# A bidirectional RWKV-7 layer: full-height lo products in the lora-up, lora rows in another buffer, chunk-end stores on ScalarE's queue

## The chip, the cores and the metric

One Trainium2 chip, one of its cores. The metric is device time in microseconds (us) of one execution; the kernel before took 1825.01 us as the median of three runs (1819.26 to 1827.5). The traces are of one profiled execution each.

## The reference

A layer mixes 128 context tokens and 2048 latent tokens of 1024 channels. All tokens are normalised and modulated to `h`, and one projection gives eight groups of 512 channels. Four of them (r, k, v, g_a) feed an RWKV-7 scan in both directions, the other four a gated short convolution. What the change touches are the two low-rank ("lora") paths, the decay `w` and the in-context rate `a`, each with its own weights for each direction `e`:

```
lw = tanh(einsum('btd,edl->betl', hf, decay_down))          # 64 rows for each direction
w = decay_w0 + einsum('betl,elc->betc', lw, decay_up)
decay = exp(-exp(-softplus(-w) - 0.5))
la = einsum('btd,edl->betl', hf, iclr_down)
a = sigmoid(iclr_bias + einsum('betl,elc->betc', la, iclr_up))
...
S = S * w_t - s_kk (kk_t * a_t) + v_t k_t                   # one step of the scan
```

Then come a group norm, the gates, the output projection, a residual and a final norm.

## The kernel before

**Three phases.** Phase 1 projects everything and writes the operands of the scan to HBM; phase 2 runs the scans in chunks of 64 tokens; phase 3 is the output projection. Nearly all the change lies in phase 1.

**Phase 1.** Tokens lie in six blocks `j` of 384 columns (the last has 256), two blocks to a "third" (`THIRD`). In a third, the loop over the four channel groups `g` of 128 takes two turns: `turn(0, g)` runs `mixA` (k, r, both loras) and a part of the convolution, `turn(1, g)` runs `gateA` (v, g_a) and the rest. `load_w` brings one weight block and splits it into a high and a low part in a rounded fp32 type (`F32R`), and `dense` sums 24 matmuls over the three useful products of high and low parts. `part_sum` does the same with a block of ones (`pss`, `psb`).

**The lora rows.** `lora_down` makes, for each block, four tiles `lw`: index `which*2 + d` for the path `which` (0 decay, 1 rate) and the direction `d`. Of the 128 rows of a tile, the 64 of half `d` hold the high part of the lora rows and the other 64 their low part. ScalarE evacuates the product to `lf`; VectorE casts and subtracts it into `lw` (L563, L564). `lf` lies in the buffer with the tag `sq`, of which there is one; `mixA` holds it from the square of k (L348) to the last product that reads `kkn` (L403).

**The lora-up.** `lup(which)` makes one output tile `up` with two matmuls: the high part of the up-weights (both halves hold the same 64 rows) by all 128 rows of `lw` (L367), and the low part by the 64 high rows alone (L368). `mixA` calls it four times: w and a of direction 0, then of direction 1. That is 8 matmuls for each of 6 x 4 pairs of block and group, 24 groups of 8 and 192 in all. `load_up` splits the up-weights once, near the start.

**Stores.** `mixA` stores four operands for each direction (`spill`, L336) out of a tag `sp` with four buffers, and by L394 the decay at the end of each chunk, `pc`: 6 numbers in each of 128 rows. All go out through SP's queue, 48 of the `pc` kind. Loads go through SP too.

**Other buffers.** `smask` (L375 to L379) is the mask by which the running sums of the decay restart at every chunk. The shifted k, r and v lie in `ok`, `or` and `ov` (L328 to L330). `bsv` (L513) holds b times its gate; `pv` the rows of the vertical convolution and, in the first third, the gate rows. `q1`, two buffers, holds a scaled copy of k, r or v (L322) and of c (L457).

**What sets the order.** The framework's scheduler places all instructions of an engine in a fixed order, from the program order, the buffers and its own estimate. So a change of buffers moves instructions. HBM transfers of SP and ScalarE take turns on eight semaphores, so that a DMA can wait for the eighth DMA before it.

Of the kernel before, what the change touches and what calls it, by code (L numbers as in the profile page):

```python
# [6 lines left out]
F32 = mybir.dt.float32  # L7
F32R = mybir.dt.float32r
BF16 = mybir.dt.bfloat16
AF = mybir.ActivationFunctionType  # L10
ALU = mybir.AluOpType
# [38 lines left out]
def phase1(K):  # L50
    nc, tc, A, S = K.nc, K.tc, K.A, K.S
    V, G, P, T = nc.vector, nc.gpsimd, nc.scalar, nc.tensor
# [18 lines left out]
    V.tensor_copy(onr[:], ones[:])  # L71
    onf = cp.tile([128, 128], F32R, name="onf")
    V.tensor_scalar(onf[:], ones[:], 0.0, 1.0, ALU.mult, ALU.add)
    smask = ca.tile([128, 384], F32, name="smask")
    eps = cp.tile([128, 1], F32, name="eps")
    V.memset(eps[:], 1e-6)
    nln2 = cp.tile([128, 1], F32, name="nln2")
# [24 lines left out]
    def load_up():  # L102

        raw = ta_.tile([128, 2, 2, 512], F32, tag="x", name="upraw", bufs=1)
        for h in range(2):
            nc.sync.dma_start(raw[h * 64:h * 64 + 64], A["wup"].rearrange("n (d p) c -> p n d c", d=2))
        parts = ca.tile([128, 6, 512], F32R, tag="upx", name="ups")
        hi, lo = parts[:, 0:4].rearrange("p (n d) c -> p n d c", d=2), parts[:, 4:6]
        for n in range(2):
            V.tensor_copy(hi[:, n], raw[:, n])  # L110
            for d in range(2):
                r = slice(d * 64, d * 64 + 64)
                V.tensor_tensor(lo[r, n], raw[r, n, d], hi[r, n, d].bitcast(F32), ALU.subtract)
                up[n, d] = (hi[:, n, d], lo[:, n])

    kept = set()

# [196 lines left out]
    def shifted(ps, j, mi, g, nm, bufs=2):  # L314

        t0, n = BLK[j]
        lo = lat_off(j)
        R = (n - lo) // 64
        rp = rot(rawl, "raw")
        P.copy(rp[:, :R, 1:65], ps[:, lo:n].rearrange("p (r c) -> p r c", c=64))  # L320
        q1 = tp.tile([128, 384], F32, tag="q1", name=f"q1{nm}_{K.u()}", bufs=2)
        P.activation(q1[:, :n], ps[:, :n], AF.Identity, scale=dcol(D_MU1 + mi * 4 + g))  # L322
        s = tp.tile([128, 384], F32, tag="sh", name=f"sh{nm}_{K.u()}", bufs=2)
        G.tensor_tensor(s[:, lo:n].rearrange("p (r c) -> p r c", c=64), rp[:, :R, 0:64], rp[:, :R, 2:66], ALU.add)  # L324
        if lo:
            rc = rot(rawc, "rawc")
            P.copy(rc[:, 1:129], ps[:, 0:128])
            V.tensor_tensor(s[:, 0:128], rc[:, 0:128], rc[:, 2:130], ALU.add)  # L328
        o = ta_.tile([128, 384], F32, tag=f"o{nm}", name=f"o{nm}_{K.u()}", bufs=bufs)
        V.scalar_tensor_tensor(o[:, :n], s[:, :n], dcol(D_MUH + mi * 4 + g), q1[:, :n], ALU.mult, ALU.add)  # L330
        return o

# [5 lines left out]
    def mixA(g, j, ws, hh, lw, pre):  # L338

        t0, n = BLK[j]  # L340
        nch = n // 64
        tl = lambda tag, b=1: (tp if tag == "sg" else ta_).tile([128, 384], F32, tag=tag, name=f"{tag}_{g}_{j}_{K.u()}", bufs=b)
        wk, wr_ = ws
        psk, psr = pre or (None, None)

        kS = shifted(psk or dense(wk, hh, n, "k"), j, 1, g, "k", 1)
        sq = tl("sq")
        P.activation(sq[:, :n], kS[:, :n], AF.Square, scale=vcol(V_KK + g))  # L348
        pss = part_sum(onr, sq, n, f"s{g}_{j}")
        n2 = sq  # L350
        V.tensor_scalar(n2[:, :n], pss[:, :n], 1e-24, None, ALU.max)
        V.reciprocal(n2[:, :n], n2[:, :n])
        kk = tl("kk")
        P.activation(kk[:, :n], kS[:, :n], AF.Identity, scale=vcol(V_KK + g))
        kkn = n2
        V.tensor_tensor(kkn[:, :n], kk[:, :n], n2[:, :n], ALU.mult)
        rS = shifted(psr or dense(wr_, hh, n, "r"), j, 0, g, "r", 1)
        kds = []
        for d in range(2):
            rows = slice(d * 64, d * 64 + 64)  # L360
            cs = slice(g * 128, g * 128 + 128)

            def lup(which):
                ps = pmm.tile([128, 384], F32, tag="mm", name=f"up{which}_{K.u()}")
                hi, lo = up[which, d]
                x = lw[which * 2 + d]
                T.matmul(ps[:, :n], hi[:, cs], x[:, :n], start=True, stop=False)  # L367
                T.matmul(ps[:, :n], lo[rows, cs], x[rows, :n], start=False, stop=True)  # L368
                return ps

            psw = lup(0)
            t = tl("t", 2)
            P.activation(t[:, :n], psw[:, :n], AF.Tanh, bias=dcol(D_W0H + d * 4 + g), scale=0.5)
            V.tensor_scalar(t[:, :n], t[:, :n], -0.5 * DEC, -0.5 * DEC, ALU.mult, ALU.add)
            c = t  # L375
            if d == 0:
                V.tensor_tensor_scan(c[:, :n], smask[:, :n], t[:, :n], 0.0, ALU.mult, ALU.add)
            else:
                V.tensor_tensor_scan(c[:, :n][:, ::-1], smask[:, :n], t[:, :n][:, ::-1], 0.0, ALU.mult, ALU.add)  # L379
            pt = rot(pp[d], "pp")  # L380
            c3 = c[:, :n].rearrange("p (a b) -> p a b", b=64)
            P.activation(pt[:, :nch, 1 - d:65 - d], c3, AF.Exp)
            P.activation(c[:, :n], c[:, :n], AF.Exp, bias=nln2[:], scale=-1.0)
            psa = lup(1)
            ta = tl("ta", 2)
            P.activation(ta[:, :n], psa[:, :n], AF.Tanh, bias=dcol(D_IBH + d * 4 + g), scale=0.5)
            v3 = lambda x_: x_[:, :n].rearrange("p (a b) -> p a b", b=64)
            al = tl("sp", 4)
            V.tensor_tensor(v3(al), v3(kk), pt[:, :nch, d:64 + d], ALU.mult)
            spill(f"al{d}", g, j, al, "al")  # L390
            rh = tl("sp", 4)
            V.tensor_tensor(v3(rh), v3(rS), pt[:, :nch, 1 - d:65 - d], ALU.mult)
            spill(f"rh{d}", g, j, rh, "rh")
            nc.sync.dma_start(S[f"pc{d}"][g * 128:(g + 1) * 128, t0 // 64:t0 // 64 + nch], pt[:, :nch, 64 - 64 * d])  # L394

            kd = tl("kd", 2)
            P.activation(kd[:, :n], ta[:, :n], AF.Identity, bias=dcol(D_KA2 + g), scale=vcol(V_KA + g))
            V.tensor_tensor(kd[:, :n], kd[:, :n], kS[:, :n], ALU.mult)
            kap = tl("sp", 4)
            V.tensor_tensor(kap[:, :n], kd[:, :n], c[:, :n], ALU.mult)  # L400
            spill(f"ka{d}", g, j, kap, "kap")
            be = tl("sp", 4)
            V.scalar_tensor_tensor(be[:, :n], ta[:, :n], 1.0, kkn[:, :n], ALU.add, ALU.mult)  # L403
            V.tensor_tensor(be[:, :n], be[:, :n], c[:, :n], ALU.mult)
            spill(f"be{d}", g, j, be, "be")
            kds.append(kd)
        bs = kds[0]
        V.tensor_tensor(bs[:, :n], kds[0][:, :n], kds[1][:, :n], ALU.add)
        V.scalar_tensor_tensor(bs[:, :n], bs[:, :n], dcol(D_RKQ + g), rS[:, :n], ALU.mult, ALU.mult)
        psb = part_sum(onr, bs, n, f"b{g}_{j}")  # L410
        bsum = tl("bsum", 2)
        P.copy(bsum[:, :n], psb[:, :n])
        return bsum
# [86 lines left out]
    def gateB(g, j, ws, hh, conv):  # L500

        o, oc, back, m = conv
        t0, n = BLK[j]
# [6 lines left out]
        P.activation(sg[:, :n], psg[:, :n], AF.Tanh, scale=0.5)  # L510
        V.scalar_tensor_tensor(sg[:, :n], sg[:, :n], 1.0, psg[:, :n], ALU.add, ALU.mult)
        psb = dense(wb, hh, n, "b")
        bsv = tp.tile([128, 7, 64], F32, tag="bsv", name=f"bsv{g}_{j}", bufs=1)  # L513
        dst = S["mixT"][512 + g * 128:640 + g * 128]
        if lo:
            V.tensor_tensor(oc, oc, sg[:, 0:128], ALU.mult)
# [35 lines left out]
    def lora_down(j, wd, wi, pre):  # L552
        n = BLK[j][1]
        nm = j % 2
        lw = [ta_.tile([128, 384], F32R, tag=f"lw{i}_{nm}", name=f"lw{i}_{j}") for i in range(4)]
        for which, (w, fn) in enumerate(((wd, AF.Tanh), (wi, AF.Copy))):
            ps = pre[which] if pre else dense(w, hs[j], n, f"l{which}")
            f = ta_.tile([128, 384], F32, tag="sq", name=f"lf{which}_{j}", bufs=1)
            P.activation(f[:, :n], ps[:, :n], fn)
            for d in range(2):  # L560
                a, b = slice(d * 64, d * 64 + 64), slice(64 - d * 64, 128 - d * 64)
                t_ = lw[which * 2 + d]
                V.tensor_copy(t_[a, :n], f[a, :n])  # L563
                V.tensor_tensor(t_[b, :n], f[a, :n], t_[a, :n].bitcast(F32), ALU.subtract)  # L564
        return lw
# [7 lines left out]
    for t3, js in enumerate(THIRD):  # L573
# [5 lines left out]
        def prepare(j):  # L579
            if j not in hs:  # L580
                if t3 == 0:
                    pre[0] = psf[2:]
                    nc.sync.dma_start(smask[:], A["cst"][:, 128:512])
                run(make_h(j, xb[j]))
            lws[j] = lora_down(j, wd, wi, psf[:2] if j == 0 else None)

# [818 lines left out]
```

## Time and profile before

| what | value |
| --- | --- |
| the three runs | 1825.01 us median (1819.26 to 1827.5) |
| the profiled execution | 1824.67 us, of which span 1822.9 us |
| TensorE matmuls busy in the span (PE) | 1703.8 us, 93%, 13424 matmuls |
| VectorE (DVE) | 1216.1 us, 67% |
| ScalarE (ACT) | 822.2 us, 45% |
| GpSimd (POOL) | 584.5 us, 32% |
| mean TensorE clock granted | 0.968 |

PE is the array, PEld its weight loads, DVE VectorE, ACT ScalarE, POOL GpSimd and SPq the issue of SP's DMAs. A matmul's recorded duration overlaps the next one's, so pace is read from the distance of starts, not from durations. "Idle before" is the time an engine stood still ahead of an instruction, and the arrow names what ended it. The three thirds of phase 1 run from about 75, 410 and 745 us, and phase 2's first products start at 977 us.

### The profile page before, as it was taken

To read this page: it belongs to the slowest core of one execution; us is meant where nothing else is said; L and a number is where in the kernel's file an instruction comes from. 1 tells how busy PE (TensorE), PEld (TensorE's weight loads), DVE (VectorE), ACT (ScalarE), POOL (GpSimd) and SP (SyncE) were. 2 spreads that over 40 slices of the span, in tenths; PEclk is the share of its full clock that TensorE was granted. 3 is DMA by queue.
4 is the path that set the end of the run, shared out by engine and by line. 5 is a ranking of instruction groups with operands and counts; after the bars stand their busy time and mean duration, and the time that the engine had idled before them with its cause. 6 is when DMAs were issued, how large, how long until landed. Compare 5 with 4: busy or idle time off the path is not lost.

```text
span 1822.9 us, 35136 instructions
## 1 busy us (share of the span) xinstructions
PE 1703.8 (93%) x13424; PEld 1539.4 (84%) x13424; DVE 1216.1 (67%) x2285; ACT 822.2 (45%) x1583; POOL 584.5 (32%) x1089
## 2 busy tenths in 40 slices
PE   5899999998999999799999799899999999898998
PEld 2789889897999999699999788788888888776886
DVE  5875788756367756447764656678777878858433
ACT  4433454523144432333342366567666656543222
POOL 0011111111021110111110777867766676422221
PEclk8899999998999999899999899999999999998999
DMA  8787788755555656547668576568667765645442
GB/s 353 205 237 208 219 264 257 206 219 141 194 142 173 179 184 187 155 138 226 195 184 275 129 179 159 138 162 198 161 165 185 161 153 129 179 149 183 143 149 98
DMA packets 315817, 335.37 MB, mean 184 GB/s; under 512 B 166968, under 2 KB 263992, under 8 KB 301568
## 3 DMA queue, kind: packets, MB, share of 16 engines
q1 hardware_dynamic: 278928, 324.20, 61.3%
q10 hardware_dynamic: 35360, 4.46, 1.6%
q0 software_dynamic: 1360, 4.46, 0.7%
q8 instruction: 106, 1.74, 0.4%
q14 instruction: 63, 0.52, 0.1%
HBM read 221.22 MB, written 111.82 MB: 183 GB/s over the span
## 4 chain that ended last, share of the span: by engine, by line
PE 53%; DMA 17%; DVE 12%; POOL 8%; issue 5%; ACT 3%; SPq 1%; DVEq 0%; ACTq 0%; POOLq 0%
DMA scr_ops<-sp 5%; POOL zt L940 4%; PE psE L1012 4%; PE psu L1278 3%; PE psu L1279 3%; PE psu L1280 3%; POOL ztmp L937 3%; DMA wr<-in_win 3%; DMA ab<-scr_at 2%; PE psS L1059 2%; DMA w<-scr_q 2%; PE psG L898 2%; PE psF L898 2%; PE mmc L161 1%; PE mmc L163 1%
## 5 line engine op out<-in xcount | busy, mean ns | idle before, releaser
L940 POOL TENSOR_TENSOR zt<-zt,ztmp 128x30 f32<-128x30 f32 (+7 forms) x510 | 198.8, 390 | 38.9
L1012 PE MATMUL psE<-str,stl 128*128 128x128 f32 x1088 | 156.2, 289 | 11.3 <-DVE E L1013 10.1
L1012 PEld LDWEIGHTS psE<-str,stl 128*128 128x128 f32 x1088 | 136.0, 197 | 19.3 <-DVE E L1013 11.8
L937 POOL TENSOR_TENSOR ztmp<-ab,zt 128x60 f32<-128x60 f32 (+7 forms) x255 | 133.9, 525 | 18.6
L785 ACT COPY bd<-rr 64x512 f32<-64x512 f32 x136 | 83.9, 617 | 79.0 <-PE psF L898 26.6
L324 POOL TENSOR_TENSOR shk<-rawl 128x384 f32<-128x384 f32 (+1 forms) x24 | 21.1, 881 | 296.9 <-ACT rawl L320 296.9
L1013 DVE TENSOR_TENSOR E<-psE,msk 128x512 f32<-128x512 f32 x136 | 93.5, 688 | 29.0 <-PE psE L1012 26.8
L1025 PE MATMUL psY<-E,sv 128*64 128x64 f32 x1088 | 105.8, 234 | 0.7 <-DVE E L1013 0.4
L1059 PE MATMUL psS<-sv,E 128*64 128x64 f32 x1056 | 104.0, 236 | 2.2 <-DVE sv L1071 2.1
L898 PE MATMUL psG<-rr,bd 128*128 128x128 f32 x544 | 83.1, 296 | 23.3 <-DVE F L899 11.8
L1059 PEld LDWEIGHTS psS<-sv,E 128*64 128x64 f32 x1056 | 74.6, 139 | 31.0 <-issue 5.8
L898 PEld LDWEIGHTS psG<-rr,bd 128*128 128x128 f32 x544 | 70.7, 201 | 27.6 <-DVE F L899 12.3
L1071 DVE TENSOR_TENSOR sv<-psS,pc 64x128 f32<-64x128 f32 x254 | 72.4, 285 | 30.7 <-PE psS L1059 22.5
L1341 POOL TENSOR_TENSOR z<-z,x 128x512 f32<-128x512 f32 x32 | 42.8, 1341 | 136.9 <-DVE z L1337 100.4
L198 POOL TENSOR_TENSOR hslb<-kd,hshb 128x384 fp32r<-128x384 f32 (+1 forms) x24 | 27.4, 1143 | 175.8 <-ACT hshb L197 163.3
L1025 PEld LDWEIGHTS psY<-E,sv 128*64 128x64 f32 x1088 | 75.8, 138 | 5.5 <-issue 2.1
L898 PE MATMUL psF<-rr,bd 128*128 128x128 f32 x544 | 75.9, 283 | 2.6 <-ACT Q L785 1.9
L1001 PE MATMUL psX<-F,zb 128*128 128x128 f32 x544 | 72.0, 281 | 4.8 <-DVE E L1013 3.3
L324 POOL TENSOR_TENSOR shv<-rawl 128x384 f32<-128x384 f32 (+1 forms) x24 | 22.6, 942 | 163.7 <-ACT rawl L320 163.7
L161 PE MATMUL mmc<-h,w 128*128 128x384 f32 (+1 forms) x192 | 69.4, 362 | 3.5 <-ACT q1r L322 1.9
L1001 PEld LDWEIGHTS psX<-F,zb 128*128 128x128 f32 x544 | 64.7, 192 | 7.9 <-DVE E L1013 5.0
L898 PEld LDWEIGHTS psF<-rr,bd 128*128 128x128 f32 x544 | 65.9, 191 | 5.6 <-ACT Q L785 2.2
(314 smaller groups left out, 5424.1 us busy)
## 6 DMA issues: line engine op xcount, KB each, us to landing
w<-scr_wsp SPq DMA_DIRECT2D x68, 1024.0 KB, 7.9
scr_wsp<-w SPq DMA_DIRECT2D x34, 1024.0 KB, 6.0
rr<-scr_ops SPq DMA_DIRECT2D x64, 512.0 KB, 4.6
scr_ops<-sp SPq DMA_DIRECT2D x160, 192.0 KB, 5.3
wr<-in_win SPq DMA_DIRECT2D x34, 512.0 KB, 6.1
ab<-scr_at SPq DMA_DIRECT2D x34, 256.0 KB, 3.9
x<-in_x SPq DMA_DIRECT2D x17, 512.0 KB, 4.7
wadas<-in_wada SPq DMA_DIRECT2D x8, 1024.0 KB, 12.9
```

What stands on the lines that cost most here:

```text
L161: T.matmul(ps[:, :n], w[:, 0, k], hh[:, 0, k, :n], start=k == 0, stop=False)
L785: (V.tensor_copy if k in ON_DVE else P.copy)(dst, src)
L898: T.matmul(ps[:, i, :].rearrange("p (a b) -> p a b", b=64), w[:, u, :], x[:, :, u, :], start=True, stop=True)
L937: G.tensor_tensor(tv, ab[:, j:j + 2, j + 2:32].unsqueeze(1).broadcast_to((128, kn, 2, n)), zt[:, :kn, j:j + 2].unsqueeze(3).broadcast_to(( ...
L940: G.tensor_tensor(zt[:, :kn, j + 2:32], zt[:, :kn, j + 2:32], tv[:, :, r], ALU.subtract)
L1001: T.matmul(px[:, i, :], B.zb[:, gi, us.start + i, :], g.F[:, us.start + i, :], start=True, stop=True)
L1012: T.matmul(pe[:, i, hd, :].rearrange("p (b t) -> p b t", b=2), g.lt[:, :, hd, us.start + k + i].rearrange("p b t -> p (b t)"), g.rt[:, :, ...
L1013: V.tensor_tensor(g.E[n][:, k:k + 2].rearrange("p a b c -> p (a b) c"), pe[:].rearrange("p a b c -> p (a b) c"), B.msk[:, ME[g.d]].unsquee ...
L1025: T.matmul(ys[gi][hd * 64:(hd + 1) * 64, u, :], v[:, hd, :], e[:, hd, 64:128], start=True, stop=True)
L1059: T.matmul(sp[r, hd, :], g.E[n][:, k, hd, 0:64], sv[:, u, hd, :], start=True, stop=True)
L1071: V.tensor_tensor(dst, sp[r], B.pc[r, 2 * p:2 * p + 2, c:c + 1].broadcast_to((64, 2, 64)), ALU.mult)
L1278: T.matmul(ps[:], mh[:, n], hi[:, cs], start=start and n == 0, stop=False)
```

## The change

The lora-up's low product takes all 128 rows of `lw` and of its weights: `load_up` now makes the low part at full height, in a tile of eight instead of six blocks, with two subtractions of 128x1024 in place of four of 64x512. The result also holds the product of both low parts, which was left out before. To make room, `smask` is kept in bf16 (a raw copy is loaded into a buffer of `t` and cast), `ov` shares the buffer of `or`, and `bsv` shares that of `pv`. `lf` moves from `sq` to the two buffers of `q1`. The 48 `pc` stores go from SP's queue to ScalarE's.

```diff
-    smask = ca.tile([128, 384], F32, name="smask")
+    smask = ca.tile([128, 384], BF16, name="smask")
...
-        parts = ca.tile([128, 6, 512], F32R, tag="upx", name="ups")
-        hi, lo = parts[:, 0:4].rearrange("p (n d) c -> p n d c", d=2), parts[:, 4:6]
+        parts = ca.tile([128, 8, 512], F32R, tag="upx", name="ups")
+        hi, lo = [parts[:, i:i + 4].rearrange("p (n d) c -> p n d c", d=2) for i in (0, 4)]
         for n in range(2):
             V.tensor_copy(hi[:, n], raw[:, n])
+            V.tensor_tensor(lo[:, n], raw[:, n], hi[:, n].bitcast(F32), ALU.subtract)
             for d in range(2):
-                r = slice(d * 64, d * 64 + 64)
-                V.tensor_tensor(lo[r, n], raw[r, n, d], hi[r, n, d].bitcast(F32), ALU.subtract)
-                up[n, d] = (hi[:, n, d], lo[:, n])
+                up[n, d] = (hi[:, n, d], lo[:, n, d])
...
-        o = ta_.tile([128, 384], F32, tag=f"o{nm}", name=f"o{nm}_{K.u()}", bufs=bufs)
+        o = ta_.tile([128, 384], F32, tag="or" if nm == "v" else f"o{nm}", name=f"o{nm}_{K.u()}", bufs=bufs)
...
-                T.matmul(ps[:, :n], lo[rows, cs], x[rows, :n], start=False, stop=True)
+                T.matmul(ps[:, :n], lo[:, cs], x[:, :n], start=False, stop=True)
...
-            nc.sync.dma_start(S[f"pc{d}"][g * 128:(g + 1) * 128, t0 // 64:t0 // 64 + nch], pt[:, :nch, 64 - 64 * d])
+            nc.scalar.dma_start(S[f"pc{d}"][g * 128:(g + 1) * 128, t0 // 64:t0 // 64 + nch], pt[:, :nch, 64 - 64 * d])
...
-        bsv = tp.tile([128, 7, 64], F32, tag="bsv", name=f"bsv{g}_{j}", bufs=1)
+        bsv = tp.tile([128, 7, 64], F32, tag="pv", name=f"bsv{g}_{j}", bufs=1)
...
-            f = ta_.tile([128, 384], F32, tag="sq", name=f"lf{which}_{j}", bufs=1)
+            f = tp.tile([128, 384], F32, tag="q1", name=f"lf{which}_{j}", bufs=2)
...
-                    nc.sync.dma_start(smask[:], A["cst"][:, 128:512])
+                    mraw = ta_.tile([128, 384], F32, tag="t", name="smaskraw", bufs=2)
+                    nc.sync.dma_start(mraw[:], A["cst"][:, 128:512])
+                    V.tensor_copy(smask[:], mraw[:])
```

Two places show how the order moves; both lie where the last third's second block (256 columns) gets its lora rows, beside the first `mixA` of that third. Line numbers of the changed kernel are smaller by two there. On VectorE before, the casts and subtractions of `lw` stand behind the last products of the other block's `mixA`, each of which writes a buffer of `sp`:

```order
L389 TENSOR_TENSOR sp_4_780_6932<-kk_4_762_6852,pp_0_472 128x384
L392 TENSOR_TENSOR sp_4_781_6935<-or_6885,pp_0_472 128x384
L400 TENSOR_TENSOR sp_4_783_6942<-kd_4_782_6939,t_4_777_6921 128x384
L330 SCALAR_TENSOR_TENSOR or_7102<-shr_7100,dv,q1r_7098 128x256
L403 SCALAR_TENSOR_TENSOR sp_4_784_6945<-ta_4_779_6930,sq_4_761_6841 128x384
L404 TENSOR_TENSOR sp_4_784_6945<-sp_4_784_6945,t_4_777_6921 128x384
L563 CAST lw_5_6960<-lf_5_6989 64x256
L563 CAST lw_5_6961<-lf_5_6989 64x256
L564 TENSOR_TENSOR lw_5_6960<-lf_5_6989,lw_5_6960 64x256
L564 TENSOR_TENSOR lw_5_6961<-lf_5_6989,lw_5_6961 64x256
```

The same place on VectorE in the changed kernel:

```order
L396 TENSOR_TENSOR kd_4_782_6939<-kd_4_782_6939,ok_6839 128x384
L561 CAST lw_5_6960<-lf_5_6989 64x256
L561 CAST lw_5_6961<-lf_5_6989 64x256
L355 TENSOR_TENSOR sq_4_761_6841<-kk_4_762_6852,sq_4_761_6841 128x384
L377 SCALAR_TENSOR_TENSOR t_4_777_6921<-smask,t_4_777_6921 128x384
L398 TENSOR_TENSOR sp_4_774_6911<-kd_4_773_6908,t_4_768_6890 128x384
L561 CAST lw_5_6962<-lf_5_7020 64x256
L561 CAST lw_5_6963<-lf_5_7020 64x256
L562 TENSOR_TENSOR lw_5_6960<-lf_5_6989,lw_5_6960 64x256
L562 TENSOR_TENSOR lw_5_6961<-lf_5_6989,lw_5_6961 64x256
```

The work on `lw` has moved ahead of the second direction's four `sp` products, and its other two subtractions follow three rows later. On ScalarE before, both `lf` stand last there:

```order
L197 CAST hshb_4_6951<-kd_4_773_6908 128x384
L320 COPY rawl_463<-mmr_7072 128x4x64
L322 ACTIVATE q1r_7098<-mmr_7072,dv 128x256
L354 ACTIVATE kk_5_793_7069<-ok_7056,vec 128x256
L412 COPY bsum_4_785_6958<-psb_4_6955 128x384
L559 ACTIVATE lf_5_6989<-mml_786_6964 128x256
L559 ACTIVATE lf_5_7020<-mml_787_6995 128x256
```

On ScalarE in the changed kernel:

```order
L392 DMA scr_pc_58<-pp_0_471 128x6x1
L557 ACTIVATE lf_5_6989<-mml_786_6964 128x256
L557 ACTIVATE lf_5_7020<-mml_787_6995 128x256
L380 ACTIVATE pp_0_472<-t_4_777_6921 128x6x64
L319 COPY rawl_462<-mmk_7026 128x4x64
L381 ACTIVATE t_4_777_6921<-t_4_777_6921,nln_112 128x384
L392 DMA scr_pc_60<-pp_0_472 128x6x1
L321 ACTIVATE q1k_7052<-mmk_7026,dv 128x256
```

Both `lf` have moved up by more than ten rows, and the two `pc` stores stand in this engine's row now.

More of the change, by code (lines that the diff above doesn't have):

```diff
@@ L359, in mixA @@
         for d in range(2):
-            rows = slice(d * 64, d * 64 + 64)
             cs = slice(g * 128, g * 128 + 128)
```

## The prediction

> **What bounds the kernel.** The page says PE 93% busy, but an average over phases says little, so the first view I read is the one of busy time by stretches, for two of the three thirds, and for ten single microseconds in the second:
>
> ```profile
> core 0: us, PE busy (x) PEld busy (x) DVE busy (x) ACT busy (x) POOL busy (x), PEclk, DMA share, GB/s
> 75.00:410.00 335.00, 327.32 (x1741) 301.97 (x1741) 247.05 (x437) 148.42 (x280) 43.27 (x42) 0.98 0.78 232
> 745.00:945.00 200.00, 187.81 (x1183) 176.07 (x1183) 126.11 (x247) 77.41 (x174) 30.44 (x37) 0.96 0.62 187
> 440.00:445.00 5.00, 5.00 (x13) 3.68 (x14) 3.60 (x6) 4.85 (x10) 1.19 (x1) 0.50 0.44 62
> 445.00:450.00 5.00, 5.00 (x24) 5.00 (x23) 2.45 (x5) 1.08 (x3) 0.00 (x0) 0.77 0.46 64
> ```
>
> Columns three on are busy times with instruction counts, then the clock. PE is busy 98% and 94% of these thirds, VectorE 74% and 63%, ScalarE 44% and 39%. So phase 1 is bound by TensorE, and time can come from two things alone: fewer microseconds of matmul at a steady pace, or fewer places where it stands still or runs at half the clock. The last two rows show that there are such places: from 440 to 445 us the granted clock is 0.50, and PE counts as fully busy with 13 matmuls, where the first third holds 1741 / 67 = 26 in 5 us.
>
> The pace is read next, from the starts in the timeline of PE, around one group of eight lora-up products:
>
> ```profile
> 915.42 0.33 PE L162 MATMUL mmr<-h,w 128*128 128x384 f32 x1
> 915.60 0.34 PE L163 MATMUL mmr<-h,w 128*128 128x384 f32 x1
> 915.77 0.34 PE L367 MATMUL up<-lw,ups 128*128 128x384 f32 x1
> 916.04 0.44 PE L368 MATMUL up<-lw,ups 64*128 64x384 f32 x1
> 916.41 0.44 PE L367 MATMUL up<-lw,ups 128*128 128x384 f32 x1
> ...
> 918.63 0.44 PE L205 MATMUL pss<-hshs,onr 128*128 128x384 f32 x1
> 918.91 0.34 PE L206 MATMUL pss<-hsls,onr 128*128 128x384 f32 x1
> ```
>
> Between full-height products the starts lie 0.175 us apart. Wherever a product of 128 rows and one of 64 rows follow each other, whichever comes first, they lie 0.27 to 0.37 apart. The 64-row product isn't short; it is dear, and so is its neighbour.
>
> Last come the places where PE stands still for the lora-up. The bracket is idle time and what ended it; the rows without one are the work before the stop and the first product back at the full pace:
>
> ```profile
> 74.69 0.41 PE L367 MATMUL up<-lw,ups 128*128 128x384 f32 x1 [4.06 <-ACT t L373]
> 81.97 0.39 PE L161 MATMUL mmc<-h,w 128*128 128x384 f32 x1
> 430.40 0.33 PE L163 MATMUL mmr<-h,w 128*128 128x384 f32 x1
> 434.77 0.69 PE L367 MATMUL up<-lw,ups 128*128 128x384 f32 x1 [4.04 <-DVE lw L564]
> 438.56 0.66 PE L367 MATMUL up<-lw,ups 128*128 128x384 f32 x1 [2.48 <-DVE lw L564]
> 447.19 0.39 PE L161 MATMUL mmc<-h,w 128*128 128x384 f32 x1
> 760.47 0.44 PE L206 MATMUL psb<-hslb,onr 128*128 128x384 f32 x1 [0.63 <-POOL hslb L198]
> 771.25 0.58 PE L367 MATMUL up<-lw,ups 128*128 128x256 f32 x1 [10.34 <-DVE lw L564]
> 773.26 0.58 PE L367 MATMUL up<-lw,ups 128*128 128x256 f32 x1 [0.93 <-DVE lw L564]
> 781.87 0.34 PE L163 MATMUL mmc<-h,w 128*128 128x384 f32 x1
> ```
>
> In the second and last third both idle spells wait for `lw`, and what follows runs at half pace for some 8.6 us (438.56 to 447.19, 773.26 to 781.87). The reasons stand on ScalarE and VectorE:
>
> ```profile
> 432.87 0.49 ACT L559 ACTIVATE lf<-mml 128x384 f32<-128x384 f32 x1 [2.29 <-DVE sp L403]
> 435.91 0.49 ACT L559 ACTIVATE lf<-mml 128x384 f32<-128x384 f32 x1 [1.32 <-DVE lw L564]
> 769.67 0.38 ACT L559 ACTIVATE lf<-mml 128x256 f32<-128x256 f32 x1 [5.66 <-DVE sp L403]
> 762.54 0.56 DVE L389 TENSOR_TENSOR sp<-kk,pp 128x384 f32<-128x384 f32 x1 [3.40 <-DMA scr_ops<-sp]
> 769.07 0.56 DVE L403 SCALAR_TENSOR_TENSOR sp<-ta,sq 128x384 f32<-128x384 f32 x1 [2.23 <-DMA scr_ops<-sp]
> ```
>
> `lf` waits for L403, the last reader of `sq`; the second `lf` waits for the subtractions on the first; and L403 itself waits for a store to leave an `sp` buffer. So PE waits for a DMA of another block, through a shared buffer.
>
> **Part 1: full-height low products.** The count of products stays 192; no matmul is added. From 915.77 to 918.91 there are 9 starts: 3.14 us. At 0.175 they would take 1.58. So a group saves 1.56, wherever PE is what ends last. The timeline has 24 groups (first products at 74.69 to 933.15). Three are the stalled ones of part 2. In 13 (240.01, 347.38, 410.23, 504.52, 582.48, 659.40, 744.68, 816.44, 833.82, 865.85, 883.23, 915.77, 933.15) PE works on behind the group without waiting: 13 x 1.56 = 20. In the other eight PE soon waits for another engine anyhow, from the group of 98.43 to that of 679.67; the wait of the first of them and that of the last but one read:
>
> ```profile
> 103.02 0.44 PE L161 MATMUL mmc<-h,w 128*128 128x384 f32 x1 [0.51 <-ACT ta L386]
> 606.13 0.44 PE L161 MATMUL mmc<-h,w 128*128 128x384 f32 x1 [0.27 <-ACT q1r L322]
> ```
>
> There a faster group mostly lengthens the wait; I take 1 us for all eight, out of 0 to 8 x 1.56 = 12. Part 1: **21 us**, bounds 20 to 32, and zero if the 64 rows are not what makes the pace.
>
> The Trainium skill speaks against this part: by "TensorEngine Tiling (Array Packing)", section "When to Use Tiling", products over 64 rows should be packed by row tiling, two to the array, rather than filled up. The rows above show no such gain, since no two 64-row products are neighbours here; if one in each pair of them had run for nothing, a group would have to gain 2 x 0.175 less, and the sum would be some 7 us smaller. The same page's section "Key Properties" says that a change of tiling mode drains the engine, which is how the 0.37 beside the 0.175 would come about; the trace agrees as far as it goes.
>
> **Part 2: `lf` out of `sq`.** With two buffers of `q1` (last read on VectorE by L330, early in a `mixA`), both `lf` can follow their products at once, and the listings of the order show the casts and subtractions ahead of the second direction's `sp` products. What each stall costs, by what PE would do without it:
>
> At 430 us: next start 430.57, then 8 + 15 products up to the one at 447.19, 23 x 0.175 = 4.0: 434.6, so 12.6 us. At 760: next start 760.65, 8 products of 256 columns (0.12 each, two thirds of 0.175) and 17 others, 3.9: 764.6 against 781.87, so 17.3 us. At the start the up-weights and the first `lw` are both late on VectorE:
>
> ```profile
> 65.68 1.30 DVE L110 CAST ups<-upraw 128x1024 fp32r<-128x1024 f32 x2 [2.44 <-DMA upraw<-in_wup]
> 68.18 1.41 DVE L113 TENSOR_TENSOR ups<-upraw,ups 64x512 fp32r<-64x512 f32 x2
> ...
> L127 DVE TENSOR_TENSOR w<-wr,w 128x1024 fp32r<-128x1024 f32 x30 | 36.8, 1228 | 21.6 <-ACT w L126 21.5
> L563 DVE CAST lw<-lf 64x384 fp32r<-64x384 f32 x20 | 7.1, 354 | 14.8 <-ACT lf L559 14.4
> L564 DVE TENSOR_TENSOR lw<-lf,lw 64x384 fp32r<-64x384 f32 x20 | 11.6, 579 | 0.6
> ```
>
> Each of the first two rows stands for a pair, so the four subtractions take 2.8 us; the two of 128x1024, by the nearest row (L127), 2 x 1.23 = 2.4, are no dearer. With a second `lf`, casts and subtractions no longer take turns with ScalarE. From 65.68, VectorE then needs 1.3 and 2.4 for the up-weights, 2 x (0.35 + 0.58) for the first path's `lw` and 2 x 0.58 more for the second's: 72.4. With the last lora-up behind it at 72.6 and 12 products at the full pace, 2.1 us, PE would be at 74.7 where it was at 81.97: 7.3 us. Together 37 us.
>
> I don't book all of it. The stores that L389 and L403 waited for are still there, 3.4 and 2.2 us at one place, and once `lw` is early they end last: PE's next sums over `hslb` come from that row of work. With `lw` ready when due, the second `mixA` also starts nearer to the first, so their stores crowd. I take two thirds, **25 us**, between 0 and 37.
>
> The Trainium skill's "TensorE: Matmul & The Clock Gate", Part 1, lets the full rate come back after about 3.4 us of steady work. The trace differs: 8.6 us at half pace behind the stalls. By the rule such stretches would cost some 2 to 3 us less each and the sum be about 7 us smaller; the measured rows decide.
>
> **Part 3: `pc` stores on ScalarE's queue.** 48 stores leave SP, 48 join ScalarE:
>
> ```profile
> L394 SPq DMA_DIRECT2D scr_pc<-pp x48: 370/378/1539, 80.7 to 941.0; - x48
> L905 ACTq DMA_DIRECT2D scr_at<-dg x34: 366/366/423, 986.8 to 1531.7; - x34
> scr_ops<-sp SPq DMA_DIRECT2D x160, 192.0 KB, 5.3
> 251.10 0.55 ACT L382 ACTIVATE pp<-t 128x384 f32<-128x384 f32 x1
> 253.93 0.70 SPq L394 DMA_DIRECT2D scr_pc<-pp  x1
> ```
>
> The first two are issue rows (ns least, median, most), the third a row of the page (KB, and median us from issue to landing). Issue on ScalarE is 48 x 0.37 = 18 us over 870, on an engine busy at most 44%: hidden, like the 0.37 each that SP is spared. The delay from `pp` to the store, 2.28 us at its longest here, was SP's turn, which frees `pp` a little sooner. What could hurt is the wait: a store that waits for its semaphore's last DMA blocks ScalarE, and behind it stand the evacuations of PE's sums. Value 0, bounds +2 and the rival below.
>
> **The rest, at nothing or little.** The bf16 mask: no scan with such a mask is in the trace; a scan of 128x384 is the dearest product there and VectorE idles 26% or more, so 0, within the bounds of 48 x 0.4 us either way on VectorE (a plain 128x384 product took 0.56, as L389 shows), most of it beside PE. `ov` in the buffer of `or`, `bsv` in that of `pv`: their users run in the same fixed order on VectorE, but the products that they feed move back in PE's row by 10 to 25 places (2 to 4 us, where other products fill in): **-2 us**, bounds -15 and 0. Phase 2 reads phase 1's stores and shifts as a whole; its first products change places by some 30 rows, up to 4 us either way, taken at 0.
>
> **The sum.** 21 + 25 - 2 = 44 us. The profiled execution took 1824.67 us (span 1822.9 and 1.8 around it), 0.3 us under the median of 1825.01, so the forecast is 1824.67 - 44 = 1781 us after rounding.
>
> **The rivals.**
> *Only one of the two terms comes.* Either the lora-up gains its 21 us and the stalls only pass to the next waiter, a store of `sp` or the slow start: 1824.67 - 21 + 0 to 2 = about 1805. Or `lf` does its part and 0.37 us is no matter of 64 rows: 1824.67 - 25 + 2 = about 1802. For the first speak L389's and L403's waits; against it that both idle spells name `lw`. Against the second speaks that all full-height neighbours keep 0.175. Together 0.22.
> *Everything comes.* The stalls vanish wholly and half of the eight waiting groups gain: 20 + 4 x 1.56 + 37 - 1 = 62, about 1763. The listings speak for it, the store waits against. 0.10.
> *Given back in full.* VectorE, 74% busy in the first third, becomes what ends last at each `mixA`, since its own store waits stay: within 9 us of before. 0.07.
> *Slower: ScalarE held by stores.* In the changed program most `pc` stores carry a wait for the eighth DMA before them, and an `sp` store among them lands 5.3 us after its issue. While ScalarE stands there no sum is evacuated. Its price: 44 us / 48 = 0.9 us of lost PE time for each store is where the gain is gone; at 1.3 us, 62 us, the time would be 1843. For it: 78% DMA share in the first third. Against: by the time of a `pc`, eight other transfers are mostly long issued, and ScalarE has 56% slack. 0.05.
>
> **How the numbers follow.** The forecast (1764 to 1800) has 0.56, one term alone 0.22, everything 0.10, given back 0.07, slower 0.05. A range of 1762 to 1808 holds the first two and nearly all of the third, some 0.85, and is cut there because only the last two lie clearly beyond. A measurement of this kernel can tell about 0.5% (9 us) from no change: faster 0.88, same 0.07, slower 0.05.
>
> **What would show it.** In the profile of the changed kernel, part 1 is right if L366, the low product now of 128 rows, starts 0.175 us after L365, and the groups take 1.6 us to the next product's start. Part 2 is right if no `up` product waits over 1 us for `lw`, the clock near 440 and 775 us stays at 1.00, and `lf` waits for no `sp` product; if instead PE waits there for `hslb` or for a sum that follows a waiting `sp`, the first rival holds. Part 3 is right if ScalarE's stores stand with little idle time before the work behind them. My prediction fails most easily in the two thirds of part 2, a choice between 0 and 37 us, and if a store on ScalarE holds up a sum.

## The result and the profile after

The changed kernel takes **1795.58 us** (median of four runs, 1792.39 to 1799.98) against 1822.13 us of the kernel before on the same chip: a ratio of 0.9853, with a 95% interval of 0.9815 to 0.9892. It is faster by 27 us (20 to 34) where 44 were forecast. Run again beside other kernels, it stood at 0.9802 (0.9775 to 0.9829). The kernel before took 1822, 1817, 1815 and 1812 us on the four occasions, so kernels of different occasions are compared by their ratios to it.

The profiled execution has a span of 1798.1 us where before had 1822.9: 24.8 us less. First the steps that came as forecast. The timeline of PE around one group of lora-up products in the last third; the columns are start, duration, and the instruction:

```profile
891.55 0.33 PE L161 MATMUL mmr<-h,w 128*128 128x384 f32 x1
891.72 0.34 PE L162 MATMUL mmr<-h,w 128*128 128x384 f32 x1
891.90 0.34 PE L365 MATMUL up<-lw,ups 128*128 128x384 f32 x1
892.07 0.34 PE L366 MATMUL up<-lw,ups 128*128 128x384 f32 x1
892.25 0.34 PE L365 MATMUL up<-lw,ups 128*128 128x384 f32 x1
```

The starts lie 0.175 us apart throughout; the 0.37 is gone. Next, the same view at the three places that waited for `lw`; the bracket holds PE's idle time and what ended it:

```profile
71.91 0.41 PE L365 MATMUL up<-lw,ups 128*128 128x384 f32 x1 [1.37 <-DVE lw L562]
...
74.43 0.69 PE L365 MATMUL up<-lw,ups 128*128 128x384 f32 x1 [0.80 <-ACT t L371]
...
435.77 0.69 PE L160 MATMUL mmc<-h,w 128*128 128x384 f32 x1 [5.88 <-ACT q1r L321]
...
754.96 0.36 PE L365 MATMUL up<-lw,ups 128*128 128x256 f32 x1 [0.70 <-DVE lw L562]
```

The 10.34 us at the last third have become 0.70. In the second third PE no longer waits for `lw`, but a few products later it waits 5.88 us for `q1r`. That is the "next waiter" of the prediction, and ScalarE and VectorE show where it comes from:

```profile
429.52 0.56 DVE L398 TENSOR_TENSOR sp<-kd,t 128x384 f32<-128x384 f32 x1 [1.48 <-DMA scr_ops<-sp]
432.63 0.56 DVE L401 SCALAR_TENSOR_TENSOR sp<-ta,sq 128x384 f32<-128x384 f32 x1 [2.55 <-DMA scr_ops<-sp]
433.11 0.61 DVE L329 SCALAR_TENSOR_TENSOR ok<-shk,dv,q1k 128x384 f32<-128x384 f32 x1
433.75 0.62 ACT L347 ACTIVATE sq<-ok,vec 128x384 f32<-128x384 f32 x1 [6.28 <-DVE ok L329]
435.14 0.58 ACT L321 ACTIVATE q1r<-mmr,dv 128x384 f32<-128x384 f32 x1
```

VectorE stands still twice for a store to leave an `sp` buffer; `ok` stands behind it in VectorE's row, the square of k waits for `ok` on ScalarE, and `q1r`, which frees a sum of PE, stands behind the square. The same chain returns later, through `kd` and `hshb`:

```profile
693.50 0.56 DVE L387 TENSOR_TENSOR sp<-kk,pp 128x384 f32<-128x384 f32 x1 [7.34 <-DMA scr_ops<-sp]
695.61 0.51 ACT L196 CAST hshb<-kd 128x384 fp32r<-128x384 f32 x1 [14.57 <-DVE kd L407]
696.17 0.69 PE L204 MATMUL psb<-hshb,onr 128*128 128x384 f32 x1 [3.99 <-ACT hshb L196]
```

VectorE's waits of phase 1 that a store out of `sp` ended, first before, then after (us in total, times, longest):

```profile
DVE sp L403 <- DMA scr_ops<-sp: 27.9, 14, 3.7
DVE sp L389 <- DMA scr_ops<-sp: 22.7, 8, 4.2
DVE sp L400 <- DMA scr_ops<-sp: 11.8, 6, 3.3
DVE sp L392 <- DMA scr_ops<-sp: 3.5, 4, 2.2
```

```profile
DVE sp L387 <- DMA scr_ops<-sp: 35.1, 13, 7.3
DVE sp L401 <- DMA scr_ops<-sp: 34.6, 15, 4.1
DVE sp L398 <- DMA scr_ops<-sp: 9.7, 6, 3.9
DVE sp L390 <- DMA scr_ops<-sp: 3.7, 4, 1.2
DVE sp L442 <- DMA scr_ops<-sp: 1.0, 2, 0.8
```

66 us have become 84. The cost to PE can be summed from its timeline: of each distance between two starts I take off 0.1755 us for 384 columns (in proportion for others), and what is left is lost, be it idle, half clock or a change of height. Up to the end of phase 1's own products:

| lost PE time, us | before | after | gain | forecast |
| --- | --- | --- | --- | --- |
| the three groups that waited for `lw`, with what followed | 39.2 | 14.2 | 25.0 | 25 |
| the 13 groups with nothing waiting behind | 19.7 | 2.9 | 16.8 | 20 |
| the other eight groups | 24.9 | 23.3 | 1.6 | 1 |
| everything else | 12.1 | 29.1 | -17.0 | -2 |
| sum | 95.8 | 69.4 | 26.4 | 44 |

The gains came within some 3 us of the forecast, and 17 us were lost again at places that the change does not touch. Of the 25.0, 16.7 us came at the last third, as worked out there (17.3); the start gave 3.5 of 7.3 and the second third 4.7 of 12.6.

The 17 us are the figure of one trace. In a second trace of the same kernel (`after_again`, below, of another occasion), with VectorE's instructions in the same order, the last lora-up product starts at 896.0 us where it started at 908.9 here. PE's waits of phase 1 for `hshs` are 4.5 us there and 7.4 here, those for `hslq` 0.8 and 4.5. So some 13 us of it come and go with the execution or the chip; what sets them is not known. The kernel before has one trace only.

Behind phase 1 the time doesn't shift as a whole, as the forecast had it. Three marks: the last lora-up product, the first and the fourteenth of the 17 stores of phase 2's result. Before:

```profile
935.23 0.38 PE L368 MATMUL up<-lw,ups 64*128 64x256 f32 x1
1200.24 0.32 SPq L1134 DMA_DIRECT2D scr_mixT<-y  x1
1606.40 0.38 SPq L1134 DMA_DIRECT2D scr_mixT<-y  x1
```

After, with what stands between the first two marks:

```profile
908.86 0.28 PE L366 MATMUL up<-lw,ups 128*128 128x256 f32 x1
947.02 1.91 SPq L874 DMA_DIRECT2D rr<-scr_ops  x4
952.62 3.75 PE L898 MATMUL psF<-rr,bd 128*128 128x128 f32 x16 [6.75 <-DMA rr<-scr_ops]
1187.30 0.38 SPq L1134 DMA_DIRECT2D scr_mixT<-y  x1
1581.58 0.38 SPq L1134 DMA_DIRECT2D scr_mixT<-y  x1
```

The lead is 26.4 us at the first mark, 12.9 at the second and 24.8 at the third. `psF`, a first product of phase 2, which the order has moved some 30 products ahead, now waits 6.75 us for its load (0.6 us of such waits before), and the row of the window behind it, whose third figure from the end is the granted clock, shows PE at half speed:

```profile
950.00:955.00 5.00, 2.38 (x11) 2.41 (x12) 0.59 (x3) 2.84 (x5) 0.00 (x0) 0.50 1.06 412
```

Then phase 2 wins 12 us back: the 13 stretches between the stores take 394.3 us in place of 406.2. There VectorE waits less for a load of `w<-scr_q`, 13.6 us against 26.5.

### The profile page after: what moved, and what is told of

It reads as the page before. It is cut to its first block, busy times and chain, and to the rows that moved or that the text cites. A ratio compares the mean times of both kernels' runs of the same rounds, so it can differ in the third digit from the quotient of the medians.

```text
span 1798.1 us, 35096 instructions
## 1 busy us (share of the span) xinstructions
PE 1672.4 (93%) x13424; PEld 1536.8 (85%) x13424; DVE 1218.0 (68%) x2284; ACT 820.2 (46%) x1583; POOL 597.0 (33%) x1089
## 5 line engine op out<-in xcount | busy, mean ns | idle before, releaser
L1012 PE MATMUL psE<-str,stl 128*128 128x128 f32 x1088 | 152.2, 285 | 6.5 <-DVE E L1013 5.4
L937 POOL TENSOR_TENSOR ztmp<-ab,zt 128x60 f32<-128x60 f32 (+7 forms) x255 | 138.4, 543 | 19.2
L1013 DVE TENSOR_TENSOR E<-psE,msk 128x512 f32<-128x512 f32 x136 | 93.6, 688 | 17.7 <-PE psE L1012 15.4
L898 PE MATMUL psF<-rr,bd 128*128 128x128 f32 x544 | 80.7, 296 | 16.3 <-DVE GA L899 7.7
L1071 DVE TENSOR_TENSOR sv<-psS,pc 64x128 f32<-64x128 f32 x254 | 72.6, 286 | 30.3 <-PE psS L1059 24.2
L898 PEld LDWEIGHTS psF<-rr,bd 128*128 128x128 f32 x544 | 70.4, 203 | 19.6 <-issue 14.7
L898 PEld LDWEIGHTS psG<-rr,bd 128*128 128x128 f32 x544 | 68.8, 195 | 14.2 <-DVE F L899 9.4
L160 PE MATMUL mmc<-h,w 128*128 128x384 f32 (+1 forms) x192 | 68.0, 354 | 13.6 <-ACT q1r L321 10.0
L1001 PEld LDWEIGHTS psX<-F,zb 128*128 128x128 f32 x544 | 65.4, 193 | 12.9 <-DVE E L1013 9.8
```

The lines of the kernel that those rows point to most:

```text
L160: T.matmul(ps[:, :n], w[:, 0, k], hh[:, 0, k, :n], start=k == 0, stop=False)
L898: T.matmul(ps[:, i, :].rearrange("p (a b) -> p a b", b=64), w[:, u, :], x[:, :, u, :], start=True, stop=True)
L937: G.tensor_tensor(tv, ab[:, j:j + 2, j + 2:32].unsqueeze(1).broadcast_to((128, kn, 2, n)), zt[:, :kn, j:j + 2].unsqueeze(3).broadcast_to(( ...
L1001: T.matmul(px[:, i, :], B.zb[:, gi, us.start + i, :], g.F[:, us.start + i, :], start=True, stop=True)
L1012: T.matmul(pe[:, i, hd, :].rearrange("p (b t) -> p b t", b=2), g.lt[:, :, hd, us.start + k + i].rearrange("p b t -> p (b t)"), g.rt[:, :, ...
L1013: V.tensor_tensor(g.E[n][:, k:k + 2].rearrange("p a b c -> p (a b) c"), pe[:].rearrange("p a b c -> p (a b) c"), B.msk[:, ME[g.d]].unsquee ...
```

## The experiments

Twelve runs followed, of ten kernels; two are repeats. **First, the low product by itself.** `lo64` takes one edit of the change back:

```diff
-                T.matmul(ps[:, :n], lo[:, cs], x[:, :n], start=False, stop=True)
+                T.matmul(ps[:, :n], lo[d * 64:d * 64 + 64, cs], x[d * 64:d * 64 + 64, :n], start=False, stop=True)
```

> The changed kernel with the low product over 64 rows again (its weights stay at full height; every engine has the same instructions in the same order as in the changed kernel). Theory S (what PE gains is partly given back, since VectorE's waits for stores out of sp and what hangs on them end last once PE is faster): about 10 us slower than the changed kernel, near 1806. Theory B (the lora-up's whole pace gain of 19 us arrives, and the loss comes from the moved order and the shared buffers, which this kernel keeps): about 19 us slower, near 1815.

Measured: 0.9909 of before (0.9871 to 0.9948). Against the changed kernel's 0.9853 and 0.9802 the low product is worth 0.6 to 1.1%, 10 to 19 us: the first figure is theory S, the second B, so this run alone does not decide. Its trace shows 1.46 to 1.57 us lost again at each undisturbed group.

`lo64_pairs` changes the sequence within a pair:

```diff
+                r = slice(d * 64, d * 64 + 64)
+                two = [(hi[:, cs], x[:, :n]), (lo[r, cs], x[r, :n])]
+                for i, (l_, r_) in enumerate(two[::-1] if which else two):
+                    T.matmul(ps[:, :n], l_, r_, start=i == 0, stop=i == 1)
```

> As lo64, but the rate path issues its 64-row product first and its 128-row product second, so that two 64-row products and two 128-row products of a direction stand side by side where nothing comes between. If the change between heights is what costs 0.2 us, half of the changes go and it is some 5 to 9 us faster than lo64, with 64-row starts 0.18 us behind a 64-row neighbour. If a 64-row product is slow by itself, it equals lo64. If neighbouring 64-row products overlap, starts come under 0.175 us apart.

Measured: 0.983 (0.979 to 0.987), faster than `lo64` by 0.8%, 14 us (more than the 5 to 9), and level with the changed kernel. 13.4 us of it lie ahead of the last lora-up product (912.7 to 899.3 in the traces). A group in its timeline of PE, whose eight products stand in one row:

```profile
881.04 0.34 PE L162 MATMUL mmr<-h,w 128*128 128x384 f32 x1
881.22 2.35 PE L368 MATMUL up<-lw,ups 128*128 128x384 f32 x8
883.40 0.34 PE L204 MATMUL pss<-hshs,onr 128*128 128x384 f32 x1
```

From the group's start to the next product 2.18 us, where eight full paces are 1.40: 0.78 lost for four changes of height (high low, low high, high low, low high), against 1.56 for eight before. So a change costs 0.195 us. The single starts in this group lie 0.27, 0.29, 0.26, 0.28, 0.26, 0.28, 0.27 and 0.28 us apart: each change delays the product behind it and the one after that by some 0.1 us each, so a 64-row product starts 0.28 to 0.29 us behind its 64-row neighbour, not the 0.18 that was expected. It isn't short, and the two don't overlap.

`lfsq` is the changed kernel with `lf` back in `sq`:

```diff
-            f = tp.tile([128, 384], F32, tag="q1", name=f"lf{which}_{j}", bufs=2)
+            f = ta_.tile([128, 384], F32, tag="sq", name=f"lf{which}_{j}", bufs=1)
```

> The changed kernel with lf in the one buffer of sq again. Both theories: the three stalls for lw come back in the trace (4 to 10 us of idle PE each at the thirds, then half the clock). Theory B: 21 us slower, near 1817. Theory S: less, 12 to 16 us, near 1810, because a standing PE gives the stores time to land.

Measured: 0.9843 (0.9812 to 0.9873). Both theories fell: the stalls are back in the trace (two waits of 3.26 and 2.93 us, two of 9.94 and 1.23), and the time is that of the changed kernel. What that means is taken up below, with the order of phase 2.

`b_share` is the kernel before with the edits that make room, and nothing else (the mask in bf16, and these):

```diff
-        o = ta_.tile([128, 384], F32, tag=f"o{nm}", ...)
+        o = ta_.tile([128, 384], F32, tag="or" if nm == "v" else f"o{nm}", ...)
...
-        bsv = tp.tile([128, 7, 64], F32, tag="bsv", ...)
+        bsv = tp.tile([128, 7, 64], F32, tag="pv", ...)
```

> The kernel before with the three savings of room alone: smask in bf16, ov in the buffer of or, bsv in that of pv. The low product stays at 64 rows, lf in sq, the pc stores on SP. Theory S: 1822 us, within 4 us of before. Theory B: about 13 us slower than before, near 1835, with longer waits for psv, q1r and hshs in the trace.

Measured: 1.0008 (0.998 to 1.0036). In the kernel before, sharing buffers costs nothing that can be told, and theory B, that the 17 us come from there, has no support; whether sharing costs something once PE waits less was not run.

**Second, each term alone.** `lf_pc` is `b_share` with the low product at 128 rows and its weights to match; `after_again` is the changed kernel on the same chip.

> b_share with the low product at 128 rows: lf in sq, pc stores on SP, all engines' instructions in the order of b_share. Floor theory (the spills through four sp buffers set a pace that PE cannot beat, so the first edit gets its gain and the second finds little left): 0.985 to 0.988 of before, as lfsq. Additive theory (each edit has its own share, 10 us for the low product, 0 for lf, so 16 us belong to the pc stores): 0.994. My forecast's terms by themselves: 21 us, 0.9885.

> The changed kernel once more, so that it stands beside the others on one chip: ratio to before 0.985, within 0.003.

Measured: `lf_pc` 0.9786 (0.9761 to 0.9812), faster than any of the three had it; `after_again` 0.9802 (0.9775 to 0.9829), faster than the expected 0.982 to 0.988. Against `b_share` the edit is worth 2.2%, 40 us, and the change's other two parts add nothing to it. Of the 38.8 us between the traces of `b_share` and `lf_pc`, 24.2 lie ahead of the last lora-up (926.6 to 902.4) and 24.3 in phase 2's 13 stretches (411.5 to 387.2), less 4.7 and 4.9 lost between and behind. The expectation had all instructions in the order of `b_share`. That is not so: in phase 1 only 24 of VectorE's 1200 instructions moved, but behind it some 300 of VectorE's 1080 instructions stand elsewhere, and the first `psF` is the 281st product behind the last lora-up in `b_share` and the 251st in `lf_pc`. So by these traces 24 us belong to the low product, and the rest came with a new order of phase 2.

`b_lf` is the kernel before with `lf` in `q1`, and no other edit.

> The kernel before with lf in the two buffers of q1 and nothing else. My forecast's term alone: 25 us faster, 0.986 of before. By lo64 (0.9909): 17 us. If the stalls only pass to the next waiter: within 5 us of before.

Measured: 0.9846 (0.9804 to 0.9888): 28 us, near the forecast's 25. Its trace has the last lora-up at 904.7 us, 21.9 ahead of that of `b_share` (which is as fast as before), and gains 10.9 more behind it, again in another order. So the two terms alone give 40 and 28 us, and together 27 to 36: they are not a sum. In phase 1, against `b_share`, it is 24.2 and 21.9, and together 17.7 and 30.6 in the two traces of the changed kernel.

**Third, what takes the second one's gain.** `sp5` is the changed kernel with five buffers for `sp`; the room is one buffer of `bsum`. Five lines of the code ask for `sp`, one is shown:

```diff
-            al = tl("sp", 4)
+            al = tl("sp", 5)
...
-        bsum = tl("bsum", 2)
+        bsum = tl("bsum", 1)
```

> The changed kernel with five buffers for sp, paid for with one instead of two for bsum. Floor theory: VectorE's waits for scr_ops<-sp fall from 84 us to under 45, q1r and hshs come sooner, and the time falls by 10 to 15 us, to 0.978 of before. Rival (the waits for stores lie beside PE's work and something else, weight loads or the DMA share, is the floor): within 4 us of the changed kernel.

Measured: 0.9682 (0.9656 to 0.9709), 1760.27 us, 20 us under `after_again` on the same chip, more than the 10 to 15. VectorE's waits for stores fell from 71.5 to 44 us. By the traces 10.9 us of the gain lie ahead of the last lora-up (896.0 to 885.1) and 9.4 behind it. `pairs_sp6` spends the room of the six-block weights on two more buffers:

> lo64_pairs with the six-block weights of before, and the room spent on six sp buffers. Floor theory: VectorE's waits for sp fall below 20 us, the extra waits of PE go, and the time is 15 to 20 us under lo64_pairs, 0.973 of before. Rival: equal to lo64_pairs, 0.983.

Measured: 0.9777 (0.9749 to 0.9805), between the two theories. VectorE's waits for stores fell to 22 us in all, but the kernel is 15 us slower than `sp5` beside it, 9.6 of them ahead of the last lora-up. Its lora-up still loses 0.78 us at each undisturbed group, 19 us if all 24 paid it. So fewer waits for stores do not give time by themselves.

The last pair is `sp5_again` and `sp5_lfsq`, which is `sp5` with `lf` in `sq`:

> sp5 once more, to stand beside the next two on one chip: 0.968 of before, within 0.004.

> sp5 with lf in sq again. Beside four sp buffers, lf in q1 gained nothing (after_again 0.9802, lf_pc 0.9786). If the stores out of sp were what took its gain, it must show here: sp5_lfsq 10 to 18 us slower than sp5_again, with the waits for lw back. Rival (the stalls of lf cost nothing, because phase 2 waits for something else at its start): within 4 us.

Measured: `sp5_again` 0.9694 (0.9654 to 0.9735), `sp5_lfsq` 0.9804 (0.9764 to 0.9843). With five buffers `lf` in `q1` is worth 1.1%, 20 us; with four it is worth nothing. And without `lf` in `q1` the fifth buffer gives nothing (0.9804 against 0.9843 and 0.9786 of `lfsq` and `lf_pc`). VectorE's waits in phase 1 of `sp5_again`:

```profile
DVE sp L390 <- DMA scr_ops<-sp: 27.7, 13, 5.0
DVE lw L561 <- ACT lf L557: 13.7, 5, 3.5
DVE sp L401 <- DMA scr_ops<-sp: 7.6, 7, 2.3
DVE sp L442 <- DMA scr_ops<-sp: 4.1, 4, 1.8
DVE sp L398 <- DMA scr_ops<-sp: 2.2, 2, 1.8
DVE sp L387 <- DMA scr_ops<-sp: 0.7, 1, 0.7
```

42 us of waits for stores, where the changed kernel on the chip of the first `sp5` run had 71.5. In `sp5_lfsq` they are 46 us, as short, but PE waits for `lw` as before, 6.79 and 1.55 us at the last third.

That looks like two waits which hide each other, but the traces put most of it elsewhere. An edit in phase 1 also changes the order that the scheduler gives to phase 2. By VectorE's row behind phase 1 the kernels fall into groups: within a group at most 17 of some 1080 instructions stand elsewhere, between groups 150 or more. Times in us, from each trace:

| order behind phase 1 | kernels | to the last lora-up | from there to the end |
| --- | --- | --- | --- |
| as before | before, `b_share` | 935.2, 926.6 | 887.7, 886.4 |
| P | the changed kernel, `after_again`, `lo64`, `lo64_pairs`, `sp5_lfsq` | 908.9, 896.0, 912.7, 899.3, 894.6 | 889.2, 883.4, 890.0, 882.6, 884.8 |
| Q | `lfsq`, `lf_pc`, `sp5`, `sp5_again`, `sp5_pcsp` | 908.2, 902.4, 885.1, 884.7, 883.0 | 875.7, 871.8, 874.0, 868.8, 879.8 |
| of their own | `b_lf`, `pairs_sp6` | 904.7, 894.7 | 875.5, 880.5 |

Behind the last lora-up every trace of order Q is shorter than every trace of order P, by 12 us on the average. With four buffers `lf` in `q1` goes along with a move from Q to P, with five from P to Q. Up to the last lora-up it is worth 6.4 us with four buffers (902.4 to 896.0) and 9.9 with five (894.6 to 884.7): nearly the same. What makes 0 of the one and 20 us of the other lies behind phase 1, where the rival of `sp5_lfsq` had looked, though its 4 us are far off. No run changed the order alone, so that the order itself makes the 12 us is likely but not shown.

`sp5_pcsp` is `sp5` with the `pc` stores on SP's queue:

> sp5 with the pc stores on SP again. My forecast gave this part 0. Theory: within 4 us of sp5_again. Rival (a store on ScalarE holds up the evacuations behind it, about 0.1 to 0.2 us for each of 48): 5 to 10 us faster than sp5_again.

Measured: 0.9676 (0.9637 to 0.9715) against 0.9694: no difference that can be told, but the intervals leave some 10 us either way, so the rival's 5 to 10 us are not excluded.

## Why the prediction was right or wrong

The direction and the range held; the size was 27 us of 44, and 36 in the second run.

- **Bound.** Right: with the same products, phase 1 gains what PE loses less, 26.4 us in both the sum of lost time and the mark at the last lora-up.
- **Part 1, 21 us.** Right in mechanism and near in size: 18.4 us in the table (16.8 and 1.6). One of the 13 groups, from 345.71 us on, lost 2.9 us to waits that had been hidden. That a change of height sets the pace is shown by `lo64_pairs`. By itself, in `lf_pc`, the part is worth 24.2 us in phase 1.
- **Part 2, two thirds of 37.** 25.0 of 39.2 us came at the stalls themselves, and `b_lf` alone gave 21.9 us in phase 1. So the size was near. Of its signs, the waits for `lw` are gone but for 1.37 us at the start and 0.70 at the last third, while the clock was 0.53 from 435 to 440 us and 0.66 from 770 to 775, not 1.00. At the second third the next waiter that the prediction named, a sum behind a waiting `sp`, took most of the gain: PE's 5.88 us for `q1r`. (The prediction reads 74.69 as the first group's first product; that group starts at 69.92, and 74.69 is where it goes on after the wait. The estimate of 7.3 us was too high there: 3.5 came.)
- **The step that failed** is the term for longer waits, "-2 us, bounds -15 and 0", and with it the sum 21 + 25 - 2. It measured -17 in the traces compared above, and about -4 in the second trace of the changed kernel. I had tied it to the shared buffers and to PE's moved rows; `b_share`, which has the sharing, is no slower than before. What the runs show instead: up to the last lora-up the two terms give 24.2 and 21.9 us alone, 17.7 and 30.6 together, and 41.5 with a fifth buffer for `sp` (926.6 of `b_share` to 885.1). So each takes from the other. That the common limit is the four `sp` buffers and the 5.3 us that a store takes to land fits the rows above, VectorE's 84 us of waits and PE's 5.88 us behind them. It is argued and not shown: `sp5` also has one `bsum` buffer less and another order in phase 1, and `pairs_sp6`, with four changes of height left in each group, has fewer waits than `sp5` and more time. Nor does `sp5_again` against `sp5_lfsq` show it, since 16.0 of the 25.9 us between their traces lie behind phase 1.
- **"Phase 2 shifts as a whole", first products at 0 within 4 us.** Wrong in both halves: 13.4 us lost between the last lora-up and phase 2's first result, 12 us won in its chunks. That the two cancel is luck. Not only the first products changed places: behind phase 1 some 390 of VectorE's 1080 instructions stand elsewhere than before. What comes behind the last lora-up took 869 to 890 us in the fourteen traces and goes with this order. How an order makes its time is open.
- **Part 3 and the mask, 0.** Nothing speaks against it. The 48 issues on ScalarE took 0.366 us at the median and 0.684 at most, and none of them stands behind idle time of ScalarE in the trace of the changed kernel; the rival with ScalarE held, at 1843 us, is out. `sp5_pcsp` finds no cost, with some 10 us of room either way; `lfsq` and `lf_pc`, which differ in this queue and in the chip, stand at 0.9843 and 0.9786, hardly further apart than the changed kernel on two occasions (0.9853 and 0.9802). The scans with the bf16 mask took 0.95 us as before:

```profile
L377 DVE TENSOR_TENSOR_SCAN t<-smask,t 128x384 f32<-128x384 bf16 x20 | 19.0, 948 | 0.2
...
L392 ACTq DMA_DIRECT2D scr_pc<-pp x48: 366/366/684, 81.3 to 915.3; - x48
```

- **The rivals.** The result lies between the forecast and "only one of the two terms comes" (1802 to 1805), and that rival's mechanism, a store of `sp` as the next waiter, is what happened at the second third, by the sign that the prediction gave for it; at the last third it did not.

## What to carry to other kernels

When two edits relieve one bound engine, ask of each what waits right behind it, and do not simply add them: in phase 1 terms of 24 and 22 us made 18 to 31 together. A likely next waiter was visible before the change, as VectorE's 66 us of waits for stores out of four buffers; a fifth buffer on top of the change made the fastest versions of this study (0.968 to 0.969 of before). Where a scheduler places all instructions anew, compare stage by stage, and look at the order of the stages that the edit does not touch before giving their time to the edit. And where short products alternate with full ones, reorder before padding: half the changes of height went with a different sequence and no memory, and that comparison kept VectorE's order throughout.

## What the runs showed that was not expected

- A change between 128-row and 64-row products cost 0.195 us, half at the product behind it and half at the next, and 64-row neighbours over the same rows did not overlap: 1.56 us for eight changes, 0.78 for four, with 384 columns as with 256. The Trainium skill's "TensorEngine Tiling (Array Packing)", section "Key Properties", has it that a change of tiling mode drains the engine. The runs agree that a change has a price; whether it is a drain they don't show.
- The stretch at half clock behind a stall varied: 8.6 us in the stalls of before, about 4 us behind the wait at 435.77 (to 439.8) and 6 us behind the one at 952.62.
- In phase 2 one and the same product of VectorE (L1130, in `b_share` L1132, 128x512) took 0.69 us in most chunks of `lf_pc`, and 1.46 to 1.93 us in four chunks of `b_share` in a row. What it met there wasn't tried.
